# Two seams of a gated feed-forward layer reordered: where the gated blocks are reloaded, and what runs before the row sums

## The chip, the cores and the metric

The kernel runs on one core of one Trainium2 chip. Its time is device microseconds from launch to end; lower is better. Three runs of the kernel before took 1679.43, 1683.52 and 1685.3 us; the median, 1683.52, is what a changed kernel is compared with.

## The reference, cut to what matters

One decoder layer for 1024 prompt tokens and 8 single-token sample sequences (1032 columns in all), model width 1024. A convolution branch and an attention branch are merged and projected back; then comes the part that the change touches:

```python
x1 = x + merged @ w_out                      # out-projection, residual
h2 = rms_norm(x1, g_ffn)                     # the row sums: mean of x1^2 over 1024 channels
z = h2 @ w_up                                # 1032 x 1024  @  1024 x 5632
z = causal_dwconv(z, width 3)                # per channel: this token and the two before it
g, v = split(z)                              # 2816 channels each = 22 blocks of 128
y = x1 + (silu(g) * v) @ w_down              # 1032 x 2816  @  2816 x 1024
out = rms_norm(y, g_final)
```

All in float32. The caches of keys and values (some 16 MB each) are also copied, shifted, to the outputs.

## The kernel before, in words

Channels lie on the 128 partitions, tokens along the free axis. A float32 product is three matmuls, since each operand is split into a rounded part and a rest (`hi` and `lo` of a weight, `h` and `l` of an input): h with hi, l with hi, h with lo. `split` makes the rounded part on ScalarE and the rest on VectorE. TensorE does nothing but matmuls, so the kernel's length is nearly the sum of them, and a moment in which TensorE waits is lost.

The stages around the change, in the order of time:

- **Out-projection (`xo`).** Output blocks 0 to 4 first. Blocks 5, 6 and 7 (`END`) are done third of the tokens by third (344 tokens; `xo_0`, `xo_1`, `xo_2`), each block added by VectorE to the residual x1 (`xr`), which is squared and summed; from the sums comes a row of scales (`rows2`) for that third, and then 8 scaled blocks, each split again into h2 (in the buffers `mh` and `ml`).
- **Plain up-projections.** Blocks ug0, uv0, ug1 (`up_0` to `up_2` by thirds of the tokens) and uv1 (all tokens). The convolution (`narrow_conv`: one ScalarE pass, three VectorE passes) and the gate (`gated`: SiLU on ScalarE, product on VectorE) turn a block pair into a gated block, which a DMA on POOL's queue stores to the scratch `g_dram[j]`.
- **Strassen pairs.** The other 20 pairs of blocks (j = 2 to 21; one ug and one uv each) are computed as a Strassen-like scheme: 7 products of 24 matmuls of 128x258 instead of 8. Inputs are sums of halves (`T2`, `T7`, `T4`, `T5`, `B11`, `B21`, `B22`). Weights for a pair are loaded as `sa` (SP's queue, then an accumulating DMA of POOL), `ra`, and `hi_wd`, `lo_wd` (both DMAs of POOL, with a ScalarE negation between). Three PSUM accumulators, `qa`, `qb` and `qc`, are evacuated into `s1`, `s2`, `s4` in between; a next product that adds onto an accumulator has to wait for that evacuation. Then convolution, gate and store, as above.
- **Down-projection (`dn`).** The 22 gated blocks are reloaded (`g`, SP's queue) and split into `gh` and `gl` in chunks of 4, 7, 7 and 4. For each chunk and each of the 8 output blocks, 36 (4 blocks) or 63 (7 blocks) matmuls of 128x344 are summed in PSUM and added by VectorE into `xs`, which is reloaded from the scratch of x1.

Instructions of one engine run in the order of its queue, and SP issues loads in the order of its queue: an instruction that waits for a buffer holds all behind it. A list scheduler orders the instructions of every engine by code order, data dependence and priority (`tc.high_priority(n)` lets a piece go ahead of up to n earlier places). Buffers of one pool tag or slot are reused in turn, so a load into a buffer waits for its last reader.

Copies of the caches (1 MB each: `o_k`, `o_v`) are paced by `paced`, one after every third weight load (`PACE`); they go through SP's queue also.

The lines that the change and the prediction's steps touch: `load_g` and the loop of loads before `down(0)` (L1119 and L1140 to L1147), the `xs` loads in `down_jobs` (L1134), the products in `strassen_pair` (L1088 to L1101), the plain convolutions (L996, L997 and L1026), the `up` loop (L990 to L994), the split helper (L68), the load helper (L174), the copies (L200).

Of the kernel before, what the change touches and what calls it, by code (L numbers as in the profile page):

```python
# [77 lines left out]
def trunk_step(ctx: ExitStack, tc: tile.TileContext, A: dict):  # L78
# [116 lines left out]
    def paced(d):  # L195

        n_weights[0] += 1
        if n_weights[0] % PACE == 0 and cache_jobs:
            dst, s = cache_jobs.pop(0)
            after(d, nc.sync.dma_start(dst, s))  # L200

    def product(ps, w, off, xh, xl, c, ks=None, late=False):
# [750 lines left out]
    for c in range(NC3):  # L953
        ps = wide(f"xo_{c}")
        for i, j in enumerate(END):
            w, off, _, _ = last[i]
            product(ps[:, i, :], w, off, mh, ml, c)
# [5 lines left out]
        for k in range(KB):  # L963
            xk = x1[k][:, cs(c)]
            nc.vector.scalar_tensor_tensor(xk, xk, pv[:, G_FFN, k:k + 1], rows2[:, cs(c)], ALU.mult, ALU.mult)
            split(xk, h2h[k][:, cs(c)], h2l[k][:, cs(c)])
# [37 lines left out]
    for i in range(4):
        b11, b12 = half(x1[i], 0), half(x1[i], 1)
        b21, b22 = half(x1[i + 4], 0), half(x1[i + 4], 1)
        f7, f2, f4 = (ph[0].tile([P, HT], F32, tag=n, name=f"{n}t{i}") for n in ("s1", "s2", "s4"))
        nc.vector.tensor_tensor(out=f7, in0=b22, in1=b12, op=ALU.subtract)  # L1010
        nc.vector.scalar_tensor_tensor(f2, f7, -1.0, b11, ALU.mult, ALU.subtract)
        nc.vector.scalar_tensor_tensor(f4, f2, -1.0, b21, ALU.mult, ALU.subtract)
        nc.vector.tensor_tensor(out=half(t5[i // 2], i % 2), in0=b11, in1=b12, op=ALU.subtract)
        for f, to, n in ((f2, T2, "t2"), (f7, T7, "t7"), (f4, T4, "t4")):
            t = slot(f"{n}{i}", F32R)
            split(f, half(t, 0), half(t, 1))
            to.append(t)

    w, off, _, _ = load_w(A["w_up"][3], "uv1"), 0, None, None
    zv = big("uv1z")  # L1020

    def ev_plain(ps):
        nc.scalar.activation(v3(zv), ps, AF.Copy)

    mm_wide([(w, 0, "uv1", ev_plain)], h2h, h2l, ONE)
# [53 lines left out]
    def v2(ap):  # L1079
        return ap.rearrange("p (a b) -> p a b", a=2)  # L1080

    def strassen_pair(j):
        w1, w2, w3, w4 = pair_weights(j)
        a, b, c = (psb[0].tile([P, 2, 512], F32, tag="q", name=f"q{n}{j}", bufs=4) for n in "abc")
        pa, pb, pc = (t[:, :, :SUB] for t in (a, b, c))
        s1, s2, s4 = (ph[0].tile([P, HT], F32, tag=n, name=f"{n}_{j}") for n in ("s1", "s2", "s4"))
        zg, zv = big(f"ug{j}z"), big(f"uv{j}z")
        strassen_product(b, w1, 4, B11, True)  # L1088
        nc.scalar.activation(v2(s1), pb, AF.Copy)
        strassen_product(a, w1, 0, B21, True)  # L1090
# [3 lines left out]
        strassen_product(c, w2, 0, T5, True)
        nc.scalar.activation(v2(s4), pc, AF.Copy)
        strassen_product(b, w3, 4, T7, False)
        nc.vector.scalar_tensor_tensor(v2(half(zv, 1)), pb, -1.0, v2(s4), ALU.mult, ALU.subtract)
        strassen_product(c, w3, 0, B22, False)
        nc.vector.tensor_tensor(out=v2(half(zg, 1)), in0=pc, in1=v2(s2), op=ALU.add)
        strassen_product(b, w4, 0, T4, False)  # L1100
        nc.scalar.activation(v2(half(zv, 0)), pb, AF.Copy, scale=-1.0)  # L1101
# [16 lines left out]
    def load_g(j):
        g = slot(f"g{j}")  # L1119
        nc.sync.dma_start(g, g_dram[j])  # L1120
        gh[j], gl[j] = slot(f"gh{j}", F32R), ph[0].tile([P, T], F32R, tag="gl", name=f"gl{j}", bufs=7)
        split(g, gh[j], gl[j])

    def down_jobs(ci):
        a, b = CHUNKS[ci]
# [246 lines left out]
```

## Time and profile before

| | |
|---|---|
| median of three runs | 1683.52 us |
| the profiled execution | 1681.59 us |
| its span, first to last instruction | 1679.8 us |
| mean granted TensorE clock | 0.988 of full |
| PE busy | 1624.3 us, 97% of the span |
| DVE, ACT, POOL busy | 67%, 36%, 11% |
| chain that ended last, by engine | PE 84%, DMA 6%, DVE 4%, issue 2%, ACT 2% |

The profile is of one execution, so its own time stands beside its span. PE's busy share is the first thing to look at: with 97% there is little idle time in all, and what there is stands in a few places. The granted clock is the second: where the clock shows 0.5, a matmul takes twice as long, and PE is "busy" all the same.

### The profile page before, as it was taken

What the parts mean: (1) busy time and instruction counts of PE and PEld (TensorE: products, weight loads), DVE (VectorE), ACT (ScalarE), POOL (GpSimd) and SP (SyncE); (2) the same over time, 40 slices, a digit from 0 to 9 for tenths busy, and PEclk for the clock granted to TensorE, in tenths of its full rate; (3) what the DMA queues carried; (4) which work ended last, traced back from release to release, by engine and by line L of the source; (5) the groups of instructions that cost most, each with busy time, mean ns of one, the idle gap of its engine ahead of it and who ended that gap; (6) DMA issues with size and microseconds to landing.
All of it is one profiled execution on the core that took longest, in us unless ns stands there. A gap on an engine that the chain in (4) does not pass through costs nothing.

```text
span 1679.8 us, 26846 instructions
## 1 busy us (share of the span) xinstructions
PE 1624.3 (97%) x11044; PEld 1577.4 (94%) x11044; DVE 1125.7 (67%) x1746; ACT 608.2 (36%) x1077; POOL 177.8 (11%) x269
## 2 busy tenths in 40 slices
PE   8999999999999999999999989999999995999997
PEld 8999998898898999999999989999999994999997
DVE  5889998798896996754346866666666664424246
ACT  6411123344433324542224544444444443201023
POOL 0101011011111102210001011111111110000002
PEclk9999999999999999999999999999999997999999
DMA  8543322332335438793543065665665748433212
GB/s 295 186 127 127 118 89 80 99 104 64 104 135 169 156 134 292 201 369 124 222 153 112 13 170 133 176 176 131 183 172 128 197 119 314 152 105 107 90 32 101
DMA packets 86986, 250.19 MB, mean 149 GB/s; under 512 B 10128, under 2 KB 31664, under 8 KB 86864
## 3 DMA queue, kind: packets, MB, share of 16 engines
q1 hardware_dynamic: 57984, 157.85, 28.2%
q0 software_dynamic: 28880, 90.64, 18.8%
q8 instruction: 86, 1.41, 0.3%
q14 instruction: 36, 0.29, 0.1%
HBM read 201.11 MB, written 92.46 MB: 175 GB/s over the span
## 4 chain that ended last, share of the span: by engine, by line
PE 84%; DMA 6%; DVE 4%; issue 2%; ACT 2%; SPq 0%; DVEq 0%; POOL 0%; POOLq 0%; ACTq 0%
PE dn L214 12%; PE qb L1076 10%; PE ga L214 6%; PE oa L214 5%; PE gb L214 5%; PE xo L214 5%; PE qc L1076 5%; PE v L214 4%; PE k L214 4%; PE q L214 4%; PE al L214 4%; PE ag L214 3%; PE first L214 3%; DMA sa<-w_ups 3%; PE qa L1076 2%
## 5 line engine op out<-in xcount | busy, mean ns | idle before, releaser
L500 DVE SCALAR_TENSOR_TENSOR ca<-cu,c_w_dw,ca 128x1019 f32<-128x1019 f32 (+22 forms) x240 | 300.8, 1269 | 1.7
L214 PE MATMUL dn<-gh,hi_wd 128*128 128x344 f32 x456 | 147.1, 324 | 19.8 <-DVE xs L932 10.2
L214 PE MATMUL dn<-gl,hi_wd 128*128 128x344 f32 x456 | 148.4, 325 | 2.9 <-DVE gl L68 2.9
L214 PE MATMUL dn<-gh,lo_wd 128*128 128x344 f32 x456 | 147.2, 323 | 0.0
L932 DVE TENSOR_TENSOR xs<-dn,xs 128x1032 f32<-128x1032 f32 x26 | 32.0, 1232 | 136.1 <-PE dn L214 124.9
L214 PEld LDWEIGHTS dn<-gh,hi_wd 128*128 128x128 f32 x456 | 86.8, 191 | 20.4 <-issue 10.5
L214 PEld LDWEIGHTS dn<-gl,hi_wd 128*128 128x128 f32 x456 | 87.0, 191 | 5.7 <-DVE gl L68 5.7
L1055 DVE TENSOR_TENSOR sb<-sa,raw_ra 128x512 f32<-128x512 f32 x20 | 13.9, 693 | 116.3 <-DMA sa<-w_ups 114.5
L214 PEld LDWEIGHTS dn<-gh,lo_wd 128*128 128x128 f32 x456 | 87.0, 191 | 0.0
L68 ACT ACTIVATE hi_wd<-raw_wd 128x896 fp32r<-128x896 f32 (+1 forms) x24 | 23.7, 988 | 154.8 <-PE dn L214 140.8
L1076 PE MATMUL qb<-t,hi_wc 128*128 128x258 f32 x320 | 61.5, 293 | 5.8 <-ACT s L1093 5.8
L214 PE MATMUL ga<-hh,lo_ga 128*128 128x344 f32 x192 | 62.5, 325 | 0.0
L214 PE MATMUL ga<-hh,hi_ga 128*128 128x344 f32 x192 | 62.4, 325 | 0.0
L214 PE MATMUL ga<-hl,hi_ga 128*128 128x344 f32 x192 | 62.3, 325 | 0.0
L214 PE MATMUL gb<-hl,hi_gb 128*128 128x344 f32 x192 | 62.0, 323 | 0.0
L214 PE MATMUL xo<-mh,hi_wo 128*128 128x344 f32 x192 | 61.8, 322 | 0.0
L214 PE MATMUL gb<-hh,lo_gb 128*128 128x344 f32 x192 | 61.8, 322 | 0.0
L214 PE MATMUL xo<-ml,hi_wo 128*128 128x344 f32 x192 | 61.8, 322 | 0.0
L214 PE MATMUL xo<-mh,lo_wo 128*128 128x344 f32 x192 | 61.6, 321 | 0.0
L214 PE MATMUL oa<-sl,hi_wco 128*128 128x344 f32 x192 | 61.5, 320 | 0.0
L214 PE MATMUL oa<-sh,lo_wco 128*128 128x344 f32 x192 | 61.5, 320 | 0.0
L214 PE MATMUL gb<-hh,hi_gb 128*128 128x344 f32 x192 | 61.1, 318 | 0.0
(810 smaller groups left out, 5426.3 us busy)
## 6 DMA issues: line engine op xcount, KB each, us to landing
o_k<-cache_k SPq DMA_DIRECT2D x16, 1023.5 KB, 7.7
o_v<-cache_v SPq DMA_DIRECT2D x16, 1023.5 KB, 7.2
g<-g_dram SPq DMA_DIRECT2D x22, 516.0 KB, 8.3
sa<-w_ups SPq DMA_DIRECT2D x20, 512.0 KB, 3.7
sa<-w_ups POOLq DMA_DIRECT2D x20, 512.0 KB, 5.7
raw_ra<-w_ups SPq DMA_DIRECT2D x20, 512.0 KB, 3.6
raw_wd<-w_down SPq DMA_DIRECT2D x16, 448.0 KB, 3.2
hi_wd<-w_ups POOLq DMA_DIRECT2D x20, 256.0 KB, 3.3
```

The source lines that it names most:

```text
L68: ins = op(*args, **kwargs)
L214: ins = nc.tensor.matmul(ps[:, :m], wk, xk, start=(k == 0 and i == 0), stop=(k == n - 1 and i == 2))
L500: after(anchor[0], nc.vector.scalar_tensor_tensor(acc[:, d:SEQ], u[:, :SEQ - d], w[:, 30 - d:31 - d], acc[:, d:SEQ], ALU.mult, ALU.add))
L932: nc.vector.tensor_tensor(out=v3(t), in0=ps, in1=v3(t), op=ALU.add)
L1055: nc.vector.tensor_tensor(out=s2, in0=s1, in1=ra[:, 512:], op=ALU.add)
L1076: nc.tensor.matmul(ps[:, s, :SUB], wk, xk, start=(first and k == 0 and i == 0), stop=(k == 3 and i == 2), skip_group_check=True)
```

## The change

Two seams are rewritten: that from the out-projection over the plain blocks into the first Strassen pair, and that from the last pair into the down-projection. What is moved:

- The matmuls of `up` are tied behind the last matmul of `xo` (`behind=last_xo`), and in the norm of a third the split of block k-1 is written behind the scaling of block k.
- Convolution and gate of the plain blocks are written at the end of the first pair (`plain_conv`), and the building of the `T` sums gets priority.
- In the first pair, the product with `B22` goes into `qc` early and is evacuated to SBUF (`c12`), and the product with `T5` gets an accumulator of its own, `qd`; two VectorE adds onto `c12` in SBUF replace the adding in PSUM.
- In the last pair the product order in the code is changed, and the loads and splits of gated blocks 0 to 3 are written inside it, with `gl0` to `gl3` in other buffers.
- The negation and the accumulating DMA of `lo_wd` lose their priority in all pairs.
- In the down-projection, the load of `xs` for a block is written one block ahead, and one gated block of the next chunk is loaded per output block instead of all ahead of the chunk.
- The cache copies pause from pair 20 to the end of the first chunk's code, and then follow every weight load instead of every third.

```diff
@@ product
+            after(behind, ins)
@@ up loop
-    zs = [slot(f"{name}z") for _, name in plain[:3]]
+    zs = [big(f"{name}z") for _, name in plain]
     ...
-            product(ps[:, i, :], ws[i], 0, h2h, h2l, c)
+            product(ps[:, i, :], ws[i], 0, h2h, h2l, c, behind=last_xo)
-    accs = [narrow_conv(o, z, big(f"{name}c")) for (o, name), z in zip(plain, zs)]
-    gated(0, *accs[:2])
@@ T sums
+    with tc.high_priority(2 * EARLY):
...
-    gated(1, accs[2], narrow_conv(NPAIR + 1, zv, slot("uv1c")))
+    def plain_conv(j):
+        gated(j, *[narrow_conv(plain[i][0], zs[i], slot(f"{plain[i][1]}c")) for i in (2 * j, 2 * j + 1)])
@@ pair_weights
-        with tc.high_priority(EARLY):
-            nc.scalar.activation(w4[1], w4[0].bitcast(F32), AF.Copy, scale=-1.0)
-            nc.gpsimd.dma_start(w4[1], src[:, 1536:], accum_op=ALU.add)
+        nc.scalar.activation(w4[1], w4[0].bitcast(F32), AF.Copy, scale=-1.0)
+        nc.gpsimd.dma_start(w4[1], src[:, 1536:], accum_op=ALU.add)
@@ strassen_pair
+        if first:
+            q3(True)
+            nc.scalar.activation(c12, pc, AF.Copy)
+            c = psb[0].tile([P, 2, 512], F32, tag="q", name=f"qd{j}", bufs=4)
...
+        elif last:
+            q7()
+            for i in range(CHUNKS[0][1]):
+                load_g(i)
+            q4()
+            q5()
+            nc.vector.tensor_tensor(out=c22, in0=c22, in1=v2(s4), op=ALU.subtract)
+            q3(False)
+            nc.vector.tensor_tensor(out=c12, in0=pc, in1=v2(s2), op=ALU.add)
...
+        if first:
+            plain_conv(0)
+            plain_conv(1)
@@ pairs and down
     for j in range(PLAIN, NPAIR):
+        if j == NPAIR - 2:
+            pace[0] = 1000
         strassen_pair(j)
...
+                load_x1(o)
                 yield w, (o % per) * nk, f"dn{ci}{o}", add_to(x1[o])
+                load_x1(o + 1)
...
-    for j in range(CHUNKS[0][1]):
-        load_g(j)
     for ci in range(len(CHUNKS) - 1):
-        for j in range(*CHUNKS[ci + 1]):
-            load_g(j)
         down(ci)
```

The order of instructions shows what the scheduler makes of it. First SP's queue at the second seam. `raw_wd00` to `raw_wd03` are the four loads of down weights of chunk 0 and `raw_wd10` the first of chunk 1; `g0` is the reload of gated block 0, `sa21` a weight of the last pair, `xs0` a residual block. Before:

```order
L1046 DMA sa21_13477<-w_ups 128x1024
L174 DMA raw_wd01_13866<-w_down 128x1024
L174 DMA raw_wd02_13952<-w_down 128x1024
L174 DMA raw_wd03_14038<-w_down 128x1024
L200 DMA o_v2048<-cache_v2048 128x2047
L1120 DMA g0_13713<-g_dram0_7828 128x1032
L174 DMA raw_wd10_14167<-w_down 128x896
L1120 DMA g1_13719<-g_dram1_7829 128x1032
```

And after the change:

```order
L175 DMA raw_wd01_13834<-w_down 128x1024
L1085 DMA g0_13616<-g_dram0_7828 128x1032
L1085 DMA g1_13622<-g_dram1_7829 128x1032
L175 DMA raw_wd02_13932<-w_down 128x1024
L1085 DMA g2_13628<-g_dram2_7830 128x1032
L175 DMA raw_wd03_14030<-w_down 128x1024
L1085 DMA g3_13634<-g_dram3_7831 128x1032
L175 DMA raw_wd10_14126<-w_down 128x896
L201 DMA o_v2048<-cache_v2048 128x2047
L1177 DMA xs0_13746<-x1_dram0_7820 128x1032
```

`g0` and `g1` stand ahead of the third weight load, `g2` and `g3` between the loads that they used to follow, and the copy stands behind them. `xs0` stood behind ten gated blocks and stands now behind four.

Next ScalarE's queue in the last pair (`s2`, `s4`: evacuations of `qb` and `qc`; `uv21z`: of `qb`; `gh0`: the rounded part of gated block 0; `hi_wd00`: that of `raw_wd00`). Before:

```order
L1093 ACTIVATE s2_21_13510<-qb21_13507 128x516
L68 ACTIVATE hi_wd00_13781<-raw_wd00_13779 128x1024
L1095 ACTIVATE s4_21_13511<-qc21_13508 128x516
L68 ACTIVATE hi_wd01_13868<-raw_wd01_13866 128x1024
L973 ACTIVATE ug21c_13689<-ug21z_13512,c_b_fdw_792,c_w_fdw_790 128x1032
L68 ACTIVATE hi_wd02_13954<-raw_wd02_13952 128x1024
L1101 ACTIVATE uv21z_13513<-qb21_13507 128x516
```

And after the change:

```order
L1128 ACTIVATE s2_21_13512<-qb21_13509 128x516
L68 ACTIVATE gh0_13618<-g0_13616 128x1032
L68 ACTIVATE hi_wd00_13742<-raw_wd00_13740 128x1024
L1105 ACTIVATE s4_21_13513<-qc21_13510 128x516
L1110 ACTIVATE uv21z_13515<-qb21_13509 128x516
L68 ACTIVATE gh1_13624<-g1_13622 128x1032
L68 ACTIVATE hi_wd01_13836<-raw_wd01_13834 128x1024
L68 ACTIVATE gh2_13630<-g2_13628 128x1032
L68 ACTIVATE hi_wd02_13934<-raw_wd02_13932 128x1024
L1116 ACTIVATE uv21z_13515<-qb21_13509 128x516
```

The split of `g0` now stands between the evacuations `s2` and `s4`, and a second evacuation into `uv21z` is new. PE's own order in the last pair is word for word the one of before, with the product of `T4` last, though the code writes it earlier.

Last, ScalarE's queue in the first pair, pair 2. Before:

```order
L973 ACTIVATE uv1c_9130<-uv1z_9055,c_b_fdw_792,c_w_fdw_790 128x1032
L1089 ACTIVATE s1_2_9184<-qb2_9182 128x516
L982 ACTIVATE ug1c_8974<-ug1c_8974 128x1032
L1065 ACTIVATE lo_wd2_9177<-hi_wd2_9176 128x512
L1093 ACTIVATE s2_2_9185<-qb2_9182 128x516
```

And after the change:

```order
L1119 ACTIVATE s1_2_9154<-qb2_9152 128x516
L977 ACTIVATE ug1c_9352<-ug1z_8733,c_b_fdw_792,c_w_fdw_790 128x1032
L1124 ACTIVATE ug2z_9157<-qc2_9153 128x516
L1066 ACTIVATE lo_wd2_9147<-hi_wd2_9146 128x512
L977 ACTIVATE uv1c_9358<-uv1z_8734,c_b_fdw_792,c_w_fdw_790 128x1032
L986 ACTIVATE ug1c_9352<-ug1c_9352 128x1032
L1128 ACTIVATE s2_2_9155<-qb2_9152 128x516
```

The evacuation `s2` keeps its place behind `lo_wd2` and gets two more instructions ahead of it, `uv1c` and the SiLU of `ug1c`.

On PE, the last third of the out-projection used to have ten matmuls of `up_0` between the block of `wo6` and that of `wo7`; all of `up_0` now stands behind `wo7`.

## Rows read from the trace of the kernel before

**Rows 1.** Page, parts 1 and 2: PE's busy share, and the granted clock by slices.

```profile
PE 1624.3 (97%) x11044; PEld 1577.4 (94%) x11044; DVE 1125.7 (67%) x1746; ACT 608.2 (36%) x1077; POOL 177.8 (11%) x269
...
PEclk9999999999999999999999999999999997999999
```

**Rows 2.** Waits of PE, 860 to 1040 us.

```profile
PE qb L1076 <- ACT s L1093: 4.1, 2, 3.8
PE up L214 <- DVE ml L68: 1.9, 1, 1.9
PE qb L1076 <- ACT s L1089: 1.3, 1, 1.3
PE qb L1076 <- ACT ug1z L994: 1.0, 1, 1.0
```

**Rows 3.** Timeline of PE around the second seam: start, duration, instruction, [idle before <-releaser].

```profile
1384.39 0.28 PE L1076 MATMUL qb<-t,lo_wd 128*128 128x258 f32 x1
...
1394.19 0.65 PE L214 MATMUL dn<-gh,hi_wd 128*128 128x344 f32 x1 [9.52 <-ACT gh L68]
...
1420.66 0.62 PE L214 MATMUL dn<-gh,hi_wd 128*128 128x344 f32 x1 [10.24 <-DVE xs L932]
```

**Rows 4.** Timeline of DVE: evacuations of the fourth, fifth and tenth down block.

```profile
1433.91 1.23 DVE L932 TENSOR_TENSOR xs<-dn,xs 128x1032 f32<-128x1032 f32 x1 [4.46 <-PE dn L214]
...
1439.61 1.23 DVE L932 TENSOR_TENSOR xs<-dn,xs 128x1032 f32<-128x1032 f32 x1 [3.46 <-PE dn L214]
...
1476.98 1.23 DVE L932 TENSOR_TENSOR xs<-dn,xs 128x1032 f32<-128x1032 f32 x1 [7.07 <-PE dn L214]
```

**Rows 5.** Windows: PE, PEld, DVE, ACT, POOL busy, PEclk, DMA share, GB/s.

```profile
1390.00:1400.00 10.00, 5.16 (x15) 3.99 (x16) 5.15 (x5) 3.62 (x4) 0.54 (x1) 0.50 1.01 382
...
1420.00:1430.00 10.00, 9.34 (x49) 9.37 (x50) 2.98 (x3) 0.41 (x1) 0.00 (x0) 0.79 1.02 412
```

**Rows 6.** Timeline of SP's queue from 1358 us.

```profile
1360.46 23.91 SPq L174 DMA_DIRECT2D raw_wd<-w_down  x3
1384.42 0.52 SPq L200 DMA_DIRECT2D o_v<-cache_v  x1
1385.04 0.54 SPq L1120 DMA_DIRECT2D g<-g_dram  x1
```

**Rows 7.** DMA issues near 1385, 1413 and 1455 us: KB, us to landing.

```profile
g<-g_dram SPq DMA_DIRECT2D x1, 516.0 KB, 8.0
...
g<-g_dram SPq DMA_DIRECT2D x1, 516.0 KB, 4.5
...
g<-g_dram SPq DMA_DIRECT2D x1, 516.0 KB, 3.1
```

**Rows 8.** Chain of waits, 1360 to 1470 us: start, duration, what.

```profile
1371.13 2.89 PE qb L1076 x24
...
1386.47 1.23 DVE lo_wd L68
...
1389.33 10.21 DMA g<-g_dram
...
1413.54 5.72 DMA xs<-x_dram
```

**Rows 9.** Timeline of ACT in the last pair.

```profile
1375.96 1.06 ACT L68 ACTIVATE hi_wd<-raw_wd 128x1024 fp32r<-128x1024 f32 x1 [1.07 <-PE qc L1076]
1376.92 0.59 ACT L1095 ACTIVATE s<-qc 128x516 f32<-128x516 f32 x1
```

**Rows 10.** Timeline of DVE, then of ACT, at the first seam.

```profile
909.15 0.51 DVE L958 TENSOR_TENSOR xr<-xo,xr 128x344 f32<-128x344 f32 x1
...
980.01 0.63 ACT L1065 ACTIVATE lo_wd<-hi_wd 128x512 fp32r<-128x512 f32 x1 [5.27 <-DMA hi_wd<-w_ups]
```

**Rows 11.** DMA issues near 965 and 1001 us.

```profile
g_dram<-uv0c POOLq DMA_DIRECT2D x1, 516.0 KB, 5.2
...
g_dram<-uv2c POOLq DMA_DIRECT2D x1, 516.0 KB, 8.0
```

More of the change, by code (lines that the diff above doesn't have):

```diff
@@ L197, in paced, with product @@
         n_weights[0] += 1
-        if n_weights[0] % PACE == 0 and cache_jobs:
+        if n_weights[0] % pace[0] == 0 and cache_jobs:
             dst, s = cache_jobs.pop(0)
             after(d, nc.sync.dma_start(dst, s))
-    def product(ps, w, off, xh, xl, c, ks=None, late=False):
+    def product(ps, w, off, xh, xl, c, ks=None, late=False, behind=None):
         n = len(xh)
@@ L956, in trunk_step @@
             w, off, _, _ = last[i]
-            product(ps[:, i, :], w, off, mh, ml, c)
+            last_xo = product(ps[:, i, :], w, off, mh, ml, c)
             nc.vector.tensor_tensor(out=x1[j][:, cs(c)], in0=ps[:, i, :CW], in1=x1[j][:, cs(c)], op=ALU.add)
@@ L962, in trunk_step @@
         nc.scalar.activation(rows2[:, cs(c)], spread(r, f"n2{c}"), AF.Copy)
[L963 to L966, printed above, removed]
+        for k in range(KB + 1):
+            if k < KB:
+                xk = x1[k][:, cs(c)]
+                nc.vector.scalar_tensor_tensor(xk, xk, pv[:, G_FFN, k:k + 1], rows2[:, cs(c)], ALU.mult, ALU.mult)
+            if k:
+                split(x1[k - 1][:, cs(c)], h2h[k - 1][:, cs(c)], h2l[k - 1][:, cs(c)])
     def big(name):
@@ L1005, in trunk_step @@
     T2, T7, T4 = [], [], []
[L1006 to L1020, printed above, removed]
+    with tc.high_priority(2 * EARLY):
+        for i in range(4):
+            b11, b12 = half(x1[i], 0), half(x1[i], 1)
+            b21, b22 = half(x1[i + 4], 0), half(x1[i + 4], 1)
+            f7, f2, f4 = (ph[0].tile([P, HT], F32, tag=n, name=f"{n}t{i}") for n in ("s1", "s2", "s4"))
+            nc.vector.tensor_tensor(out=f7, in0=b22, in1=b12, op=ALU.subtract)
+            nc.vector.scalar_tensor_tensor(f2, f7, -1.0, b11, ALU.mult, ALU.subtract)
+            nc.vector.scalar_tensor_tensor(f4, f2, -1.0, b21, ALU.mult, ALU.subtract)
+            nc.vector.tensor_tensor(out=half(t5[i // 2], i % 2), in0=b11, in1=b12, op=ALU.subtract)
+            for f, to, n in ((f2, T2, "t2"), (f7, T7, "t7"), (f4, T4, "t4")):
+                t = slot(f"{n}{i}", F32R)
+                split(f, half(t, 0), half(t, 1))
+                to.append(t)
     def ev_plain(ps):
-        nc.scalar.activation(v3(zv), ps, AF.Copy)
-    mm_wide([(w, 0, "uv1", ev_plain)], h2h, h2l, ONE)
-    gated(1, accs[2], narrow_conv(NPAIR + 1, zv, slot("uv1c")))
+        nc.scalar.activation(v3(zs[3]), ps, AF.Copy)
+    mm_wide([(load_w(A["w_up"][3], "uv1"), 0, "uv1", ev_plain)], h2h, h2l, ONE)
     for i in range(4):
         split(half(t5[i // 2], i % 2), half(h2h[i], 1), half(h2l[i], 1))
+    def plain_conv(j):
+        gated(j, *[narrow_conv(plain[i][0], zs[i], slot(f"{plain[i][1]}c")) for i in (2 * j, 2 * j + 1)])
     def rows_of(tiles):
@@ L1077, in strassen_product, with load_g @@
                                      stop=(k == 3 and i == 2), skip_group_check=True)
-    def v2(ap):
-        return ap.rearrange("p (a b) -> p a b", a=2)
+    gh, gl = [None] * NPAIR, [None] * NPAIR
+    def load_g(j):
+        g = slot(f"g{j}")
+        nc.sync.dma_start(g, g_dram[j])
+        gh[j] = slot(f"gh{j}", F32R)
+        gl[j] = slot(f"gl{j}", F32R) if j < CHUNKS[0][1] else ph[0].tile([P, T], F32R, tag="gl", name=f"gl{j}", bufs=7)
+        split(g, gh[j], gl[j])
     def strassen_pair(j):
@@ L1087, in strassen_pair, with q3, q5, q7 @@
         zg, zv = big(f"ug{j}z"), big(f"uv{j}z")
+        first, last = j == PLAIN, j == NPAIR - 1
+        c11, c12, c21, c22 = v2(half(zg, 0)), v2(half(zg, 1)), v2(half(zv, 0)), v2(half(zv, 1))
+        def q3(new):
+            strassen_product(c, w3, 0, B22, new)
+        def q5():
+            strassen_product(c, w2, 0, T5, True)
+            nc.scalar.activation(v2(s4), pc, AF.Copy)
+        def q7():
+            strassen_product(b, w3, 4, T7, False)
+            if last:
+                nc.scalar.activation(c22, pb, AF.Copy, scale=-1.0)
+            else:
+                nc.vector.scalar_tensor_tensor(c22, pb, -1.0, v2(s4), ALU.mult, ALU.subtract)
+        def q4():
+            strassen_product(b, w4, 0, T4, False)
+            nc.scalar.activation(c21, pb, AF.Copy, scale=-1.0)
         strassen_product(b, w1, 4, B11, True)
@@ L1090, in strassen_pair @@
         strassen_product(a, w1, 0, B21, True)
-        nc.vector.tensor_tensor(out=v2(half(zg, 0)), in0=pa, in1=v2(s1), op=ALU.add)
+        nc.vector.tensor_tensor(out=c11, in0=pa, in1=v2(s1), op=ALU.add)
+        if first:
+            q3(True)
+            nc.scalar.activation(c12, pc, AF.Copy)
+            c = psb[0].tile([P, 2, 512], F32, tag="q", name=f"qd{j}", bufs=4)
+            pc = c[:, :, :SUB]
         strassen_product(b, w2, 4, T2, False)
         nc.scalar.activation(v2(s2), pb, AF.Copy)
[L1094 to L1101, printed above, removed]
+        if first:
+            nc.vector.tensor_tensor(out=c12, in0=c12, in1=v2(s2), op=ALU.add)
+            strassen_product(c, w2, 0, T5, True)
+            nc.scalar.activation(v2(s4), pc, AF.Copy)
+            nc.vector.tensor_tensor(out=c12, in0=c12, in1=v2(s4), op=ALU.add)
+            q7()
+            q4()
+        elif last:
+            q7()
+            for i in range(CHUNKS[0][1]):
+                load_g(i)
+            q4()
+            q5()
+            nc.vector.tensor_tensor(out=c22, in0=c22, in1=v2(s4), op=ALU.subtract)
+            q3(False)
+            nc.vector.tensor_tensor(out=c12, in0=pc, in1=v2(s2), op=ALU.add)
+        else:
+            q5()
+            q7()
+            q3(False)
+            nc.vector.tensor_tensor(out=c12, in0=pc, in1=v2(s2), op=ALU.add)
+            q4()
+        if first:
+            plain_conv(0)
+            plain_conv(1)
         ga = narrow_conv(j, zg, slot(f"ug{j}c"))
@@ L1113, in trunk_step, with load_x1 @@
     ph[0].release()
-    ph[0] = ctx.enter_context(tc.tile_pool(name="ph2", bufs=2))
-    gh, gl = [None] * NPAIR, [None] * NPAIR
+    ph[0] = ctx.enter_context(tc.tile_pool(name="ph2", bufs=2, reuse_waits="tile"))
     x1 = [None] * KB
[L1118 to L1122, printed above, removed]
+    def load_x1(o):
+        if o < KB and x1[o] is None:
+            x1[o] = slot(f"xs{o}")
+            nc.sync.dma_start(x1[o], x1_dram[o])
     def down_jobs(ci):
@@ L1131, in down_jobs @@
             for o in range(oo * per, oo * per + per):
-                if x1[o] is None:
-                    x1[o] = slot(f"xs{o}")
-                    nc.sync.dma_start(x1[o], x1_dram[o])
+                load_x1(o)
                 yield w, (o % per) * nk, f"dn{ci}{o}", add_to(x1[o])
+                load_x1(o + 1)
     def down(ci):
         a, b = CHUNKS[ci]
-        for job in down_jobs(ci):
+        nxt = deque(range(*CHUNKS[ci + 1]))
+        for i, job in enumerate(down_jobs(ci)):
             mm_wide([job], gh[a:b], gl[a:b], ONE)
-    for j in range(CHUNKS[0][1]):
-        load_g(j)
+            if i and nxt:
+                load_g(nxt.popleft())
+        pace[0] = 1
     for ci in range(len(CHUNKS) - 1):
-        for j in range(*CHUNKS[ci + 1]):
-            load_g(j)
         down(ci)
```

3 lines of the change are left out of this document (added).

## The prediction

> **What bounds the kernel now.** I read the page's busy shares and clock first: TensorE (PE) is busy 97% of the span, and its clock is full but for one slice near the end [rows 1]. So this is a matmul-bound kernel with some 50 us of idle time, and a change can win only where PE waits. Next I listed PE's waits in the two stretches that the diff touches. At the first seam they are small: 4.1 us for the evacuation of `qb`, 1.9 for `ml`, 1.3, 1.0 [rows 2]. At the second the timeline has two of 9.52 and 10.24 us [rows 3]. Third, the timelines of PE, DVE and SP, to see what each wait hangs on.
>
> The second seam costs the kernel 27 us, and this can be measured without adding waits. PE's last Strassen matmul ends at 1384.39 + 0.28 = 1384.67 [rows 3]. The tenth output block of the down-projection is evacuated at 1476.98, so 92.3 us lie between [rows 4]. The ten blocks are 8 x 36 + 2 x 63 = 414 matmuls. Two evacuations of 36-matmul blocks in the undisturbed stretch are 5.70 us apart [rows 4], that is 0.158 us a matmul, and 414 of them 65.4 us. The rest, 26.9 us, is: a wait of 9.52 us for the first `gh` and one of 10.24 us for the first evacuation, whose `xs` had not come [rows 3], short ones for `gl` between them, and matmuls at half speed after each wait: the clock is 0.50 in the ten us around the first start, and 0.79 after the second [rows 5].
>
> Why did both loads come late? SP's queue. Three weight loads took SP from 1360.46 to 1384.4, most of it waiting for their buffers; a cache copy followed, and `g0` left at 1385.04 [rows 6], already 0.4 us after PE had run out. It landed 8.0 us later, beside the copy, against 3.1 for a `g` alone and 4.5 for one behind a single weight load [rows 7]. The next weight load then held the queue until `lo_wd02` had been made at 1387.7, and a later `g` of the burst took 10.2 us; `xs0` stood behind ten of these and behind another held weight load, left at 1413.54 and landed 5.72 later [rows 8].
>
> **The change, part by part: the second seam.** PE's order there is not changed; only what feeds it is. `g0` may go when the T2 product has released its buffer, some nine matmuls before that product's end: the product starts at 1371.13, its 24 matmuls last 2.89 us (0.12 each) [rows 8], so 1372.9. I take 4.5 us to land (the row behind one weight load), 1377.5. From there ScalarE's queue decides, because `gh0` and `hi_wd00` now stand ahead of the evacuation `s4`: 1377.5 + 1.06 + 1.06 + 0.59 [rows 9], a `gh` taken as long as a `hi_wd`, gives `s4` done at 1380.1. Before, `s4` started at 1376.92 [rows 9]. The product with B22, which adds onto `qc`, could start after T2, T5 and T7, at 1371.1 + 2.9 + 2.1 + 2.9 = 1378.9 (T5's remainder is two us, since part of it runs earlier), so it **waits 1.2 us**: a new wait, made by the change. PE then ends the pair at 1385.9, and `gh0`, `gl0`, `gh1` are long there: the 9.5 us wait goes.
>
> What is late next: `g2` stands behind `raw_wd02`, which waits for `lo_wd00` (after `hi_wd00`, 1379.6 + 1.2), about 1381.1; so it leaves at 1381.4, lands 4.5 us later, and `gh2` and `gl2` (1.06 + 1.23) put `gl2` at 1388.4, when PE, seven matmuls into `dn00`, wants it at 1387.0: **1.4 us**. `g3` stands behind `raw_wd03`, which waits for `lo_wd01`, in the orders of ScalarE and VectorE an estimated four us after `lo_wd00`, 1385.2: it leaves at 1385.6, lands about 1390.4, and `gl3` is made by 1392.9, 2.6 us after PE has done the 20 matmuls before it: **2.6 us**. For the clock after these I take **2.0 us**: the second wait of before cost 63 - 49 = 14 matmuls in ten us of the window that holds it, less 0.66 us of idle at its start, about 1.6 us [rows 5], and there are now three smaller waits in a row. `xs0` leaves near 1390.4, behind `raw_wd10` and a copy; by the row of `g0` it lands 8.1 us later, 1398.5, and `dn00` (54 matmuls after the start, with the stalls) is complete a little after 1400: the **10.24 us wait goes**, and 0.3 us is left for the rest. Sum: 26.9 - (1.2 + 1.4 + 2.6 + 2.0 + 0.3) = **19.4 us gained**.
>
> Bounds. Nothing stalls at all: 26.9 - 0.3 = 26.6. All four `g` land in 8.0 us as `g0` did: `gh0` comes 3.5 later, the B22 product waits 4.7, and the chain `lo_wd00`, `raw_wd02`, `g2` moves by 3.5, with another 3.5 of its own; remaining 7.5 + 3.5 + 3.5 + 1.6 for the clock = 16.1, gain 10.8. I take the middle row, 4.5, since no copy is in front of these loads any more and the store `g_dram[20]` is the only large one beside them.
>
> The rule that speaks against this part is that of a queue in order. The row is `lo_wd` of pair 2 [rows 10]: ScalarE sat 5.27 us for a DMA, and the evacuation behind it, ready long before, held PE for most of the 4.1 us of [rows 2]. The Trainium skill (Perfetto Trace Analysis, Tensor Engine Instruction) says that ScalarE and VectorE are strict FIFO; the trace agrees, and by that rule `s4` pays for whatever `g0` takes: 1.2 us in the sum, 4.7 in rival A, and nothing if ScalarE could let `s4` pass.
>
> The Trainium skill (DMA: Bandwidth & Descriptors, Anatomy of one DMA) prices one DMA at about 2.0 us plus bytes over 436 GB/s. For 516 KB that is an estimate of 3.2 us, against 3.1 in the row of a lone `g` [rows 7]; with that for every `g`, each 1.3 us sooner, the three waits would shrink by 1.2, 1.3 and 1.3 and the time would be 1660. I keep 4.5, the row of a `g` with a weight in front.
>
> **The first seam.** Tying `up` behind `xo` takes ten matmuls of `up_0` (1.6 us) out of the place where PE waited for the evacuation of block 6 (909.15 + 0.51 [rows 10]) anyway: the matmuls of `wo7` cannot start before it. That is 1.9 us of PE work later than before. But what follows is timed by the row sums, and these by the same evacuations; the short waits for `up` evacuations (`ml` 1.9, `ug1z` 1.0 [rows 2]) shrink by as much, and I place the first Strassen product at 964.1, as before. In the first pair, the 1.3 us for `s1` go, as the B22 product fills in. The wait for `s2` stays: T7 comes 24 matmuls later in the order (2.9 us), but `s2` is now behind `lo_wd2` (980.01, for its DMA [rows 10]), then `uv1c`, which waits for the store of gated block 0, then a SiLU. That store leaves POOL's queue behind `hi_wd2`, about 974.7, and lands 5.2 to 8.0 us later [rows 11]: 979.9 to 982.7. With 1.2, 1.1 and 0.6 for the three ScalarE instructions T7 starts at about 984.3, in place of 981.2 (980.01 + 0.63 + 0.59), with 2.9 us more done. So **0 us**, from -2 (the store lands first, `lo_wd2` decides) to +5 (8.0 us or more, and a new half-clock stretch).
>
> **The rest.** The priority taken from `lo_wd` shows nowhere in the order of pair 21: it stands directly ahead of `s2` as before. Two added VectorE adds and one evacuation in one pair lie on engines at 67% and 36% [rows 1]. The copies paused from pair 20 come back one per weight load in the first two chunks; a job there is 9.9 us (63 x 0.158) and its DMA is one copy, one weight, one `g`, one `xs`. At the 412 GB/s of [rows 5] these 2.5 MB take 6.1 us, under 9.9: nothing, if that rate holds.
>
> **Sum.** 1681.59 (the profiled execution) - 19.4 - 0 = 1662.2. It is 1.9 us below the median of the runs, so the prediction is **1664 us**.
>
> **Rivals.** A: ScalarE's queue holds `s4` for a late `g0`, and the `g` behind it come late too, as in the upper bound: 1683.5 - 10.8 = 1672.7; for it speak the 8.0 and 10.2 us landings [rows 7, 8], against it that those shared the DMA engines with a copy or ten loads. B: everything is hidden, since the loads land in 3.1 us and the clock doesn't fall: 1683.5 - 26.6 = 1656.9; for it the lone `g`; against it that `raw_wd03` alone holds `g3`, a matter of order. C: the first seam loses 5 us (the store of block 0 late): 1669. D, slower: the bunched copies starve the weights. Each of the eleven jobs of chunks 0 and 1 that issue one would have to lose 1.8 us to give back the 19.4, that is a weight's landing has to grow beyond the 10 us that a job leaves it; for this the 10.2 us landing of a `g` in a burst, against it that weights are fetched more than one job ahead. From there it decides; at 2.5 us a job it is 27.5 - 19.4 = 8 us slower, 1692. E: the change doesn't do what it says. In part that is so (PE's products in the last pair keep their order, and `g2`, `g3` stay behind weights), and it is in the sum.
>
> **Chances.** The forecast 0.64, its own range 1659 to 1668; A 0.15, B 0.08, C 0.06, D 0.04, and 0.03 for a gain eaten up within 5 us by A, C and D together. The range that leaves out no more than two in ten, with the bounds: 1656 to 1674. A measurement of this kernel tells about 0.3%, 5 us, from nothing. Faster 0.93, same 0.03, slower 0.04.
>
> **What would show it.** Right: PE's wait for `gh` at the start of `dn` gone, waits of 1 to 3 us for `gl` in its place, no wait for `xs`, the pair's end near 1386, T7 of pair 2 near 984, the tenth evacuation near 1457.5 where it was 1476.98 [rows 4]. Wrong: a wait of PE for `s4` over 3 us; PE waiting for `hi_wd` or `lo_wd` in chunks 0 and 1; a first Strassen product later than 966.

## The result, and the profile after

The changed kernel took 1661.4 us (median of four runs, 1660.94 to 1664.54) against 1683.0 us before (a fourth run, 1682.5, has joined the three): a ratio of 0.9878, 95% interval 0.9856 to 0.9899. By the ratio, which is taken over all runs, that is 20.5 us less, with 17.0 and 24.2 as the ends; the medians differ by 21.6. The prediction was 1664 us, 1656 to 1674.

The profiled execution is the slowest of the four, 1664.54 us with a span of 1662.8, so its span lies 17.0 us under that of before. Where these 17.0 come from can be read by lining up fixed instructions of the two traces. The fifth evacuation of the out-projection comes at 874.15 before and at 875.39 after: this execution began 1.2 us late, long ahead of the change. From there to the T2 product of the last pair it is 496.82 us before and 497.15 after: **the first seam and the pairs together cost 0.3**. From T2 to the tenth down evacuation it is 106.0 before and 86.7 after: **the second seam gives 19.3**. The tail costs 0.7. This distance, from T2 to the tenth evacuation, is used below for every run, since it doesn't move with how an execution starts: with all its matmuls back to back it would be 79.3 us (113 matmuls of 0.12, 414 of 0.158, and 0.3 to 0.4 for the last one's end), so 26.7 us were lost in it before, and 7.4 are now.

The distance begins and ends with these lines of the timelines of PE and DVE, first of before, then of after (start, duration, instruction; the end of before is in [rows 4]):

```profile
1370.97 0.41 PE L1076 MATMUL qb<-t,hi_wb 128*128 128x258 f32 x2
```

```profile
1372.54 0.41 PE L1077 MATMUL qb<-t,hi_wb 128*128 128x258 f32 x2
...
1459.28 1.23 DVE L934 TENSOR_TENSOR xs<-dn,xs 128x1032 f32<-128x1032 f32 x1 [2.88 <-PE dn L215]
```

The page of the changed kernel answers [rows 1]. PE's share is one point up, and the slice in which the clock was 0.7 is gone:

```profile
PE 1622.7 (98%) x11044; PEld 1576.3 (95%) x11044; DVE 1125.7 (68%) x1747; ACT 608.1 (37%) x1079; POOL 178.4 (11%) x269
...
PEclk9999999999999999999999999999999999999999
```

PE's timeline at the second seam answers [rows 3]. The last Strassen matmul and the first down matmul are 0.12 us apart, and neither of the two long waits is there; in brackets stand the four short ones that are left:

```profile
1381.80 0.39 PE L1077 MATMUL qc<-mh,hi_wc 128*128 128x258 f32 x1 [1.33 <-ACT s L1105]
...
1387.51 0.28 PE L1077 MATMUL qb<-t,lo_wd 128*128 128x258 f32 x1
1387.63 0.32 PE L215 MATMUL dn<-gh,hi_wd 128*128 128x344 f32 x1
...
1389.90 0.42 PE L215 MATMUL dn<-gh,hi_wd 128*128 128x344 f32 x1 [1.17 <-ACT gh L68]
1391.17 0.42 PE L215 MATMUL dn<-gl,hi_wd 128*128 128x344 f32 x1 [0.85 <-DVE gl L68]
...
1395.27 0.66 PE L215 MATMUL dn<-gl,hi_wd 128*128 128x344 f32 x1 [0.33 <-DVE gl L68]
```

SP's timeline answers [rows 6]. `g0` and `g1` leave at 1374.5, 13 us before PE needs them; `g2` and `g3` each stand 0.4 us behind a weight load that had waited for its buffer:

```profile
1374.54 1.04 SPq L1085 DMA_DIRECT2D g<-g_dram  x2
1382.75 0.33 SPq L175 DMA_DIRECT2D raw_wd<-w_down  x1
1383.17 0.38 SPq L1085 DMA_DIRECT2D g<-g_dram  x1
1387.20 0.33 SPq L175 DMA_DIRECT2D raw_wd<-w_down  x1
1387.63 0.38 SPq L1085 DMA_DIRECT2D g<-g_dram  x1
```

Their landings, and that of `xs0` behind a weight and a copy, answer [rows 7] (issues near 1374, 1383 and 1393 us; of the first two `g0` took 4.7 and `g1` 5.8, and `g3`, issued at 1387.6, took 5.2):

```profile
g<-g_dram SPq DMA_DIRECT2D x2, 516.0 KB, 5.2
...
g<-g_dram SPq DMA_DIRECT2D x1, 516.0 KB, 5.6
...
xs<-x_dram SPq DMA_DIRECT2D x1, 516.0 KB, 8.6
```

PE no longer waits for `xs`. VectorE does, 1.74 us ahead of the first evacuation, as its timeline shows:

```profile
1402.00 1.23 DVE L934 TENSOR_TENSOR xs<-dn,xs 128x1032 f32<-128x1032 f32 x1 [1.74 <-DMA xs<-x_dram]
```

ScalarE's timeline answers [rows 9]. It sat 2.73 us for `g0`, and the evacuation `s4`, two places behind, came at 1381.17:

```profile
1375.93 0.59 ACT L1128 ACTIVATE s<-qb 128x516 f32<-128x516 f32 x1
1379.25 1.07 ACT L68 ACTIVATE gh<-g 128x1032 fp32r<-128x1032 f32 x1 [2.73 <-DMA g<-g_dram]
1380.22 1.04 ACT L68 ACTIVATE hi_wd<-raw_wd 128x1024 fp32r<-128x1024 f32 x1
1381.17 0.58 ACT L1105 ACTIVATE s<-qc 128x516 f32<-128x516 f32 x1
```

The window after the start of the down-projection answers [rows 5]; its granted clock is 0.66 in place of 0.50:

```profile
1390.00:1400.00 10.00, 8.79 (x33) 7.67 (x34) 8.27 (x9) 5.46 (x6) 0.00 (x0) 0.66 0.87 316
```

At the first seam PE's waits answer [rows 2]. The waits for `ml` and `s1` are gone, and longer ones for `xr` and `s2` stand in their place:

```profile
PE qb L1077 <- ACT s L1128: 5.7, 2, 5.2
PE xo L215 <- DVE xr L960: 3.3, 1, 3.3
PE qb L1077 <- DMA lo_wd<-w_ups: 1.2, 1, 1.2
```

ScalarE's timeline answers [rows 10]: ahead of `s2` it waited for `hi_wd2`, and then for the store of gated block 0:

```profile
981.56 0.63 ACT L1066 ACTIVATE lo_wd<-hi_wd 128x512 fp32r<-128x512 f32 x1 [4.83 <-DMA hi_wd<-w_ups]
982.90 1.25 ACT L977 ACTIVATE uv1c<-uv1z,c_b_fdw,c_w_fdw 128x1032 f32<-128x1032 f32 x1 [0.71 <-DMA g_dram<-uv0c]
```

### The profile page after: what moved, and what is told of

The parts are those of the page before. It is cut to its first block, busy times and chain, and to the rows that moved or that the text cites. A ratio compares the mean times of both kernels' runs of the same rounds, so it can differ in the third digit from the quotient of the medians.

```text
span 1662.8 us, 26829 instructions
## 1 busy us (share of the span) xinstructions
PE 1622.7 (98%) x11044; PEld 1576.3 (95%) x11044; DVE 1125.7 (68%) x1747; ACT 608.1 (37%) x1079; POOL 178.4 (11%) x269
## 4 chain that ended last, share of the span: by engine, by line
PE 85%; DMA 7%; DVE 3%; ACT 2%; issue 2%; SPq 0%; POOL 0%; DVEq 0%; POOLq 0%; ACTq 0%
PE dn L215 13%; PE qb L1077 9%; PE ga L215 6%; PE oa L215 5%; PE gb L215 5%; PE xo L215 5%; PE v L215 4%; PE k L215 4%; PE q L215 4%; PE qc L1077 4%; PE al L215 4%; DMA sa<-w_ups 3%; PE ag L215 3%; PE first L215 3%; PE qa L1077 2%; PE s L612 2%
```

## The experiments

The distance is the one defined above, from each run's profile; the ratio is to the kernel before, run on the same chip. Its medians beside the other runs were 1680.3 to 1682.8 us, so times are compared by the ratio. The distance scatters too: the run with `s2` early has the changed kernel's orders at the second seam and differs from it by 1.6 us, and the three runs with both orders lie 1.8 us apart.

| run | time, us | ratio, 95% interval | distance, us |
|---|---|---|---|
| before | 1683.0 | 1 | 106.0 |
| changed | 1661.4 | 0.9878 (0.9856, 0.9899) | 86.7 |
| second seam only | 1663.5 | 0.9883 (0.9864, 0.9903) | 85.8 |
| first seam only | 1681.7 | 1.0002 (0.9989, 1.0015) | 106.4 |
| copies paced as before | 1669.6 | 0.9927 (0.9909, 0.9945) | 90.7 |
| gated blocks early, xs late | 1683.9 | 1.0014 (1.0003, 1.0026) | 105.4 |
| xs early, gated blocks late | 1669.1 | 0.9934 (0.9911, 0.9957) | 92.6 |
| two copies per weight | 1678.5 | 0.9986 (0.9975, 0.9998) | 100.9 |
| s4 ahead of gh0 | 1662.8 | 0.9890 (0.9865, 0.9916) | 85.3 |
| g0 to g3 in a row | 1659.7 | 0.9862 (0.9844, 0.9881) | 82.6 |
| both of these orders | 1656.6 | 0.9852 (0.9829, 0.9874) | 80.8 |
| s2 early in the first pair | 1657.2 | 0.9858 (0.9835, 0.9880) | 85.1 |
| both orders, s2 early | 1654.8 | 0.9845 (0.9830, 0.9860) | 81.1 |
| the same and a tile for xo | 1656.9 | 0.9857 (0.9836, 0.9878) | 82.6 |

**Which seam?** Each seam of the changed kernel was put back by itself. The edit for the second seam only, in short:

```diff
-            product(ps[:, i, :], ws[i], 0, h2h, h2l, c, behind=last_xo)
+            product(ps[:, i, :], ws[i], 0, h2h, h2l, c)
...
-        first, last = j == PLAIN, j == NPAIR - 1
+        first, last = False, j == NPAIR - 1
```

> The first seam is as in the kernel before, the second as in the changed one. Theory (the second seam carries the whole gain): 1661 to 1665 us, and from the start of the T2 product of the last pair to the tenth down evacuation 86 to 88 us, as in the changed kernel, against 105.9 before. Rival (the first seam gave part of it): 1668 us or more, with the same distance in the second seam.

And for the first seam only (with the loads of the down-projection as in the kernel before):

```diff
-        first, last = j == PLAIN, j == NPAIR - 1
+        first, last = j == PLAIN, False
```

> The first seam is as in the changed kernel, the second as before. Theory (the first seam is neutral): 1681 to 1686 us, the first Strassen product within 1 us of before once the start of the out-projection is lined up, T7 of pair 2 waits about 5 us for s2 in place of 3.8. Rival (the reordering of the first seam pays): 1677 us or less.

The second seam alone has the whole gain, the first alone has none: 1.0002, with the wait for `s2` at 5.3 us as expected. Both rivals fall. With the second seam only, PE's waits there are not those of the changed kernel: 1.70 us for `s4`, and 3.08 us for an evacuation into `uv21z` at the start of `dn`.

**The two orders behind the waits that are left.** With a tie between instructions, ScalarE does `s4` ahead of `gh0`, and SP loads `g0` to `g3` ahead of `raw_wd02`; first both, then each alone.

```diff
+            e4 = q5()
             for i in range(CHUNKS[0][1]):
-                load_g(i)
+                load_g(i, e4)      # split of g tied behind e4
...
+        if name in BEHIND:         # wd02, wd03, wd10: behind the load of g3
+            after(g_loads[BEHIND[name]], d)
```

> The changed kernel, with two orders tied: ScalarE evacuates s4 ahead of the split of gated block 0, and SP loads gated blocks 0 to 3 one behind the other, ahead of the third and fourth weight of chunk 0. Theory (ScalarE's queue in order makes the 1.3 us wait, SP's queue in order the waits for gh2, gl2 and gl3): all of them go and with them the half-clock stretch, 5 to 7 us less than the changed kernel, 1654 to 1657 us. Rival (the loads are slow because they share the DMA engines): four loads in a row land in 6 to 9 us each, gh0 or gl1 is waited for instead, 1660 us or more.

> The changed kernel with ScalarE's order alone tied: s4 is evacuated ahead of the split of gated block 0; SP's order of loads is the changed kernel's. The distance from the T2 product of the last pair to the tenth down evacuation is 106.0 us before, 86.7 in the changed kernel, 80.8 with both orders tied. Theory (queue in order, each wait its own term): the wait of the B22 product for s4, 1.3 us, goes, the waits for gh and gl stay: 84.5 to 86 us. Rival (the late loads all hang on ScalarE's held queue): 82 us or less.

> The changed kernel with SP's order alone tied: gated blocks 0 to 3 are loaded in a row, ahead of the third and fourth weight of chunk 0; on ScalarE the split of gated block 0 still stands ahead of s4. Theory: the waits for gh2, gl2 and gl3 and the half-clock stretch after them go, the 1.3 us for s4 stay, or grow by 1 to 2 us as four loads share the engines: 82 to 84 us of that distance. Rival (the waits for gl come from ScalarE and VectorE being late, not from the loads): 85.5 us or more.

The distance falls by 1.4 with the first order, by 4.1 with the second, by 5.9 with both. The 1.4 are within the scatter, so that these are two separate terms isn't shown. With `s4` first its wait of 1.33 us does go, but the waits for `gh` and `gl` don't stay as they were: they grow from 2.35 us to 3.90. What is shorter in this run is the stretch at half clock behind them, some 3 us in place of 6.5. PE's timeline of the run with `s4` first:

```profile
1388.78 0.58 PE L221 MATMUL dn<-gh,hi_wd 128*128 128x344 f32 x2 [0.64 <-ACT gh L1096]
1390.05 0.43 PE L221 MATMUL dn<-gl,hi_wd 128*128 128x344 f32 x1 [0.69 <-DVE gl L1097]
...
1392.82 0.57 PE L221 MATMUL dn<-gh,hi_wd 128*128 128x344 f32 x2 [1.88 <-ACT gh L1096]
1394.09 0.66 PE L221 MATMUL dn<-gl,hi_wd 128*128 128x344 f32 x1 [0.69 <-DVE gl L1097]
```

With the four loads in a row the waits for `gh` and `gl` go, and the half clock with them; 1.49 us for `s4` are left, and 1.5 us for an `xs` are new. In the run with both orders the four loads landed in 6.6 us (median; 7.6 for the last two), longer than the 4.7 to 5.8 of the changed kernel, and hid but for one wait of 0.69 us for `gl`, as the first left at 1370.5. By the times alone the changed kernel and this run can't be told apart (0.9878 and 0.9852). SP's timeline of the run with both orders:

```profile
1370.52 3.02 SPq L1091 DMA_DIRECT2D g<-g_dram  x4
1375.85 7.04 SPq L178 DMA_DIRECT2D raw_wd<-w_down  x2
```

And its DMA issues near 1372 us:

```profile
g<-g_dram SPq DMA_DIRECT2D x4, 516.0 KB, 6.6
```

**Are the two long waits separate?** The prediction priced the early `g` and the early `xs` as two terms. One was taken out at a time; both runs keep the new pace of the copies.

```diff
                 yield w, (o % per) * nk, f"dn{ci}{o}", add_to(x1[o])
-                load_x1(o + 1)
...
-            if i and nxt:
-                load_g(nxt.popleft())
...
     for ci in range(len(CHUNKS) - 1):
+        for j in range(*CHUNKS[ci + 1]):
+            load_g(j)
```

> The changed kernel without the two loading rules of the down-projection: gated blocks 0 to 3 are still loaded inside the last pair, but xs is loaded at its own job and all gated blocks of the next chunk ahead of the chunk, as before. Theory (the two waits of before are separate and each load order pays for one): the down-projection starts as early as in the changed kernel, and a wait of 7 to 11 us for xs0 comes back after two blocks; the distance is 95 to 99 us, 1669 to 1674 us. Rival (with the early start xs0 is hidden anyway): no wait for xs, 1661 to 1664 us.

That was wrong by 10 us: the early gated blocks alone gave nothing at all. The down-projection did start sooner, 15.2 us after T2 in place of 23.2, and the wait for `xs` grew from 10.2 to 16.2 us. The chain of waits of this run shows where it comes from:

```profile
1397.36 9.97 PE dn L215 x51
...
1407.35 1.06 ACT hi_wd L68
...
1408.44 1.24 DVE lo_wd L68
...
1409.69 0.33 SPq L175
...
1411.80 8.28 DMA g<-g_dram
...
1422.43 1.15 DVE xs L934
```

SP's timeline of this run, the landing of its `xs0`, and VectorE ahead of the evacuation:

```profile
1410.08 0.52 SPq L201 DMA_DIRECT2D o_v<-cache_v  x1
1410.70 1.56 SPq L1085 DMA_DIRECT2D g<-g_dram  x3
1412.35 8.07 SPq L1177 DMA_DIRECT2D xs<-x_dram  x8
...
xs<-x_dram SPq DMA_DIRECT2D x1, 516.0 KB, 9.0
...
1418.63 3.80 DVE L68 TENSOR_TENSOR gl<-g,gh 128x1032 fp32r<-128x1032 f32 x3 [6.67 <-ACT gh L68]
```

And SP's timeline of the kernel before at the same place:

```profile
1412.64 0.33 SPq L174 DMA_DIRECT2D raw_wd<-w_down  x1
1413.08 0.37 SPq L1120 DMA_DIRECT2D g<-g_dram  x1
1413.54 4.38 SPq L1134 DMA_DIRECT2D xs<-x_dram  x8
```

`xs0` stands in SP's queue behind the second weight of chunk 1. That weight's buffer comes free when the fourth weight of chunk 0 has been split, and the split's own buffer when PE has done the first two down blocks, at 1407. So the wait starts from PE's own progress: it moves with PE, and an earlier start can't hide it. That alone would have left it as long as it was. But it grew by 6.0 us, in three parts. From the weight to `xs0` SP now takes 2.66 us in place of 0.90, as a copy and three gated blocks stand between, where one block stood. `xs0` lands 9.0 us after issue in place of 5.72. And VectorE splits the three blocks before it evacuates, 1.0 us after `xs0` has landed. Of the 8.0 us by which `dn` starts sooner these 6.0 are thus given back, and 1.3 had gone before to the short waits for `gh` and `gl` and the half clock among them. How much of this the copy alone is worth no run here shows. The counterpart takes the loads of `g0` to `g3` out of the last pair again:

```diff
             q7()
-            for i in range(CHUNKS[0][1]):
-                load_g(i)
...
+    for j in range(CHUNKS[0][1]):
+        load_g(j)
     for ci in range(len(CHUNKS) - 1):
         down(ci)
```

> The counterpart of the run with gated blocks 0 to 3 loaded early and xs late, which gained nothing (its wait for xs0 grew from 10.2 to 16.2 us): here the gated blocks are loaded after the last pair, as before, but xs one job ahead and one gated block of the next chunk per job, as in the changed kernel. Theory (xs0 no longer stands behind the second weight of chunk 1, whose buffer only comes free when PE has done the first down blocks): the 9.5 us wait for gh stays, that for xs goes, the distance is 93 to 98 us (106.0 before, 86.7 changed), 1669 to 1674 us. Rival (either half alone gives nothing): a wait for xs of 8 us or more, 102 us or more, 1678 us or more.

1669.1 us, distance 92.6: the early `xs` without the early gated blocks are worth 13.4 us of the 19.3. The wait for `xs` goes, and with it the half clock that followed. The time that PE waits for `gh` does not: `dn` starts 3.7 us sooner than before, with no copy in front of `g0`, but in place of one wait of 9.52 us there are two, 9.4 together (PE's timeline of this run):

```profile
1389.18 0.94 PE L215 MATMUL dn<-gh,hi_wd 128*128 128x344 f32 x2 [5.86 <-ACT gh L68]
...
1395.52 0.94 PE L215 MATMUL dn<-gh,hi_wd 128*128 128x344 f32 x2 [3.55 <-ACT gh L68]
```

The early gated blocks add 5.9 on top of the early `xs`, and 0.7 without them.

**The cache copies.** The pause and the bunching were taken out, and then the bunching was doubled.

```diff
-            pace[0] = 1000
...
-        pace[0] = 1
```

> The changed kernel, but with the cache copies one per three weight loads throughout, as before. SP's order then has a copy ahead of the load of gated block 3. Theory (bunched copies cost nothing, a copy ahead of a load costs its landing some 3 us): block 3 lands 7 to 8 us after issue instead of 5.2, 1662 to 1667 us. Rival (the bunched copies starve the down-projection): 1658 us or less.

```diff
+        for _ in range(2 if pace[0] == 1 else 1):
             if n_weights[0] % pace[0] == 0 and cache_jobs:
```

> The changed kernel with two cache copies behind each weight load after the pause, in place of one, until the eight that are left are gone. Theory (copies cost nothing by their bytes, but a load behind them in SP's queue lands later): xs0 stands behind two copies and lands 11 to 14 us after issue, PE waits 3 to 6 us for it, distance 90 to 93 us, 1664 to 1668 us, and no wait for hi_wd or lo_wd in chunk 1. Rival A (hidden): distance under 88 us, 1662 us or less. Rival B (the weights starve): waits for hi_wd or lo_wd of 3 us or more in chunk 1, 1670 us or more.

With the old pace a copy goes out just ahead of `g3`. That landed 8.3 us after issue, a wait of 3.3 us for `gh` came with it, and the distance grew by 4.0. The timed runs lost 8.2 us, plus or minus 4.7, so more than was expected, and whether anything beyond these 4.0 belongs to it is open. So the pause is a needed part of the change: it keeps copies out of the loads that PE waits for.

With two copies per weight nearly all is lost: 1678.5 us, where 1664 to 1668 were expected. No weight starves, but `xs` behind a pair of copies land late, and PE waits 10.8 us for them in four places, where 3 to 6 us were expected, with half-clock stretches behind. The landing of the `xs` issued at 1433 us:

```profile
xs<-x_dram SPq DMA_DIRECT2D x1, 516.0 KB, 11.2
```

Two windows of this run, PE busy throughout the first and 6.64 of 10 us of the second:

```profile
1410.00:1420.00 10.00, 10.00 (x66) 10.00 (x65) 3.46 (x3) 2.02 (x2) 0.00 (x0) 1.00 1.01 333
1430.00:1440.00 10.00, 6.64 (x32) 6.67 (x33) 3.56 (x3) 1.29 (x2) 0.00 (x0) 0.83 0.97 325
```

And PE's waits for it from 1330 us to the end:

```profile
PE dn L216 <- DVE xs L935: 10.8, 4, 4.9
```

The DMA engines are full from 1400 to 1440 (shares of 0.97 to 1.01) at 325 to 352 GB/s. The mechanism of rival D is real, one copy per weight away, and its victim is the residual and not the weights.

**The first seam's own waits.** In the first pair, `hi_wd2` was put ahead of the accumulating load of `sa3` on POOL, and `s2` ahead of the SiLU and of `uv1c` on ScalarE; last, the out-projection's last block got a PSUM tile of its own.

```diff
+        if j == PLAIN + 1:
+            after(first_hi[0], acc)        # sa3 behind hi_wd2
...
-            plain_conv(1)
+            plain_conv(1, e2)              # its ScalarE passes behind s2
```

> The changed kernel with the first pair's order tied: POOL issues hi_wd2 ahead of the accumulating load of sa3, and ScalarE evacuates s2 ahead of the SiLU of ug1 and of the convolution pass of uv1. Theory (the 5.2 us wait of T7 is ScalarE's queue behind lo_wd2, uv1c and the SiLU): the wait falls under 1.5 us, the half clock from 982 to 990 goes, 5 to 8 us less than the changed kernel, 1653 to 1657 us. Rival (the reordered work only moves: the next pair waits for sa3, or T4 for lo_wd2): less than 2 us gained, 1659.5 us or more, and a wait of 3 us or more in the next 20 us.

> Both tied orders of the second seam and the tied order of the first pair (hi_wd2 and s2 ahead), without the PSUM tile of its own for the out-projection. Theory (the first pair's order is worth the 4 us by which its run lay under the changed kernel, beside the second seam's): 1651 to 1654 us. Rival (what the first pair saves is waited for again in pair 4, as its waits there suggest, and the 4 us were mostly scatter): 1655 to 1658 us, as with the second seam's orders alone (1656.6).

```diff
+            if c == NC3 - 1 and j == KB - 1:
+                ps = wide("xo_l")
             last_xo = product(ps[:, i, :], w, off, mh, ml, c)
```

> Both tied orders of the second seam, the first pair with hi_wd2 and s2 ahead, and a PSUM tile of its own for the last block of the out-projection, so that its last third need not wait for the evacuation of block 6. Theory (three separate terms): the second seam gives 5 us as measured, the first pair 2 to 4, the 3.3 us wait for xr goes with its half-clock stretch, 3 to 5 us: 1648 to 1653 us. Rival (the first seam is held by the row sums and by the weights of pairs 3 and 4, so what is saved is waited for later): 1654 to 1658 us, with new waits for ml or for s in pair 4.

The wait for `s2` of 5.2 us goes, as the theory has it. The time hardly does: PE reaches T2 of pair 4 4.3 us sooner after the first Strassen product (51.5 us in place of 55.8), and the T4 product of pair 4 only 1.5 us sooner (66.3 in place of 67.8), since it now waits in pairs 3 and 4:

```profile
PE qb L1084 <- ACT s L1135: 2.0, 1, 2.0
PE qb L1084 <- ACT hi_ra L68: 1.4, 1, 1.4
```

0.9858 and 0.9878 cannot be told apart, nor can 0.9845 and 0.9852 for the combination, so the times decide nothing. The trace speaks for the rival, most is waited for later, though no single new wait has the 3 us that it named. The PSUM tile gained nothing either: its wait for `xr` goes, and one of 3.9 us for `uv1z` and one of 3.2 us in pair 4 come in. The best version is the changed kernel with both orders and `s2` early, 1654.8 us. Its ratio lies 0.0033 under that of the changed kernel, with 0.0026 as the uncertainty; by the distance, the order of the four loads carries most of it.

## Why the prediction was right

- **Place and sign.** The gain is the second seam's, 19.3 us in the profile where 19.4 were forecast; the first seam is 0.3 us where 0 was forecast. Lined up by the fifth evacuation, the first Strassen product came 0.6 us later than before and T7 of pair 2 at 984.4, where 984.3 was forecast: `uv1c` did wait for the store of block 0.
- **The new wait for s4** was put at 1.2 us and is 1.33. The run with `s4` ahead of `gh0` takes it away; PE then waits 1.55 us longer for `gh` and `gl`, so what this wait costs by itself isn't shown.
- **The waits for g2 and g3** were put at 1.4 and 2.6 us. They are 1.17 + 0.85 and 0.33. `g2` took 5.6 us to land and `g3` 5.2, not 4.5, which made the first larger; and PE, at half clock by then, came late for `gl3`, so that the third term is small and the clock's is large.
- **The clock** was put at 2.0 us. Ten us at 0.66 are 3.4 us lost. The sum of the remainder, 7.5, was right at 7.4 because these errors cancel, and that is luck: with the same orders at this seam the run with `s2` early lost 1.7 us to the clock, and its distance is 85.1.
- **xs0** was to land at 1398.5. Lined up by T2 it landed nearly 2 us later; VectorE stood 1.74 us for it, and PE did not have to wait. So the 10.24 us went as forecast.
- **Two terms that aren't two.** The step "the 9.5 us wait goes" and the step "the 10.24 us wait goes" were added as if each had its own edit. The sum holds for both edits together; each alone is 0.7 and 13.4. The failed expectation comes from this: the wait for `xs` starts from PE's own progress, so that an earlier start of PE doesn't shorten it, and the copy and the gated blocks that now stood ahead of `xs0` lengthened it.
- **Copies.** "At 412 GB/s these 2.5 MB take 6.1 us, under 9.9" gave the right answer with a rate from loads alone: with two copies per weight the full engines moved 325 to 352 GB/s. One copy per weight is hidden, two are not. That chance, rival D, was set at 0.04 and for the wrong victim; and D counted eleven copies where SP's timeline of the changed kernel has eight.

Rival A had all four `g` land in 8 us; with no copy in front they took 4.7, 5.8, 5.6 and 5.2, and none came near the 3.2 us by which the prediction put 1660 beside its sum. With the old pace a `g` behind a copy took 8.3 and was waited for, so the rival turns in the main on where the copies are.

## What to carry to other kernels

At a seam, write down for each late load what stands ahead of it in its queue, and for each of these what it waits for. If the answer is the engine that is going to wait, an earlier start of that engine doesn't hide the load: the wait moves along with it, and grows with whatever is put between. The load has to be moved past the held instruction itself. Paced background copies belong between the loads that nobody waits for; whether more of them fit can be tried by doubling them once.

## What was not expected of the hardware

Two cache copies behind every weight kept the DMA engines at a share of 0.97 to 1.01 and moved 325 to 352 GB/s, where a burst of `g` and `xs` loads moved 412 [rows 5]. And the waits of 1.17 and 0.85 us at 1389.9 and 1391.2 were followed by half clock from 1392 to 1398.6 (matmuls of 0.49 us in place of 0.32, one every 0.29 us in place of 0.158, so 1.8 times as long and not twice), the 1.33 us wait at 1381.8 by none: the window from 1380 to 1390 has the full clock. The stretch isn't the same in every execution: with the same orders, the run with `s2` early had waits of 0.81 and 0.84 us there and some 3 us at half clock behind them.
